# Turning the probabilities of two stick-breaking pairs instead of one with VectorE and DMAs

## The chip, the cores and the metric

The kernel runs on one core of a Trainium2 chip. The metric is the device time of one execution in microseconds (us), lower being better. Before the change the median of 3 runs is 719.0 us (718.34 to 719.76).

## What is computed

A decoder trunk of two layers, for one sequence of 256 tokens of 1024 features, all in float32:

```python
proj = x @ w_in      # q,k,v of 8 stick-breaking heads | q,k,v of 8 MoBA heads | gate_sb | gate_moba
# branch A, per head: stick-breaking, causal, no softmax
z = q @ k.T * scale
log_keep = where(past, log_sigmoid(-z), 0)
suffix = cumsum(log_keep, reverse=True) - log_keep
w = where(past, exp(log_sigmoid(z) + suffix), 0);   o_sb = w @ v
# branch B, per head: with 256 tokens there is one block, so plain causal softmax attention with partial rotary
merged = sigmoid(g_sb) * (o_sb @ w_branch_sb) + sigmoid(g_moba) * (o_mb @ w_branch_moba)
x = layer_norm(ALPHA * x + merged @ w_out)
x = layer_norm(ALPHA * x + (silu(x @ w_gate) * (x @ w_up)) @ w_down)
```

## The kernel before

**Products in three parts.** Each float32 operand is held as two numbers, `hi` and `lo`, so that a product is three matmuls: hi·hi, hi·lo and lo·hi. `split_line` makes the two: ScalarE (ACT) rounds to `hi`, VectorE (DVE) subtracts to `lo`. Weights come as granules of 128 x 1024 numbers (122 a layer): a DMA on SP's queue into one of six `raw` buffers, then ACT to `whi` and DVE to `wlo`, rings of ten slots. Seven granules a layer come over POOL's queue instead. A `raw` load waits until DVE has subtracted the granule that had the buffer before. SP issues its DMAs in order, so a waiting one holds up those behind it.

**The stages of a layer**, named by the matmuls' outputs, `l0` or `l1` ahead: `pv`/`pq` (in layer 1 `pvq`) are v and q projections; `pqk` are q and k of a stick-breaking pair of heads (four pairs, 0 to 3); `pk` and `pu` are k and v of the MoBA heads; `pg` the gates; `pa` and `pb` the two branch projections, four groups each; `pw` the output projection; `pft`, `pf` and `pd` (`pe` at the very end) the feed-forward part. `bankM` hands out two PSUM banks in turn: `pg` of the first gate reuses the bank of the first `pu`, so that it waits until ACT and DVE have split that `pu` into `vmb`. The attention of both branches is woven into these projections.

**A stick-breaking pair** (`sb_line`): scores `sb_s` on TensorE (PE), the mask on DVE, two sigmoids on ACT (`keep` and `beta`), four cumulative products on DVE (`inc`), and `beta = beta * inc` on DVE, which leaves 768 probabilities in each of 128 rows (two heads, 128 + 256 keys). They have to be turned (keys on the partitions) before PE can multiply them with v. Two ways exist:

- `weighted`: six transposes of 128 x 128 on PE into PSUM (`sb_pT`), split by ACT and DVE into `pp`.
- `bounced`: `bounce_line` turns blocks of 32 x 32 on DVE, stores 384 KB to DRAM (`sb_scr`) on SP's queue, loads them back with four DMAs of 96 KB that put the blocks in their places, and ACT and DVE split the result into `pp`.

After either, `both_parts` has four matmuls (`sb_o`), two copies on ACT and four adds on DVE (`sb_f`), and the split into `osb_hi`/`osb_lo`. All pairs share one `pp`, so they pass in order. All MoBA pairs (`mb_...`) bounce; their sums go to `omb_hi`/`omb_lo`, which `pb` reads: its first half (`ks` 0 and 1) takes pairs 0 and 1, the second half pairs 2 and 3. Before the change the stick-breaking pair 3 alone bounces, in each layer.

**The order of the work** is fixed when the program is built. `Weave` keeps a modelled time for PE (`weave.t`), ACT, DVE and POOL; generators (`line()`, `sb_line`, the weight stream) yield the modelled time at which they can go on, and the next one whose time has come issues its instructions. `DMA_ISSUE`, `DMA_STORE` and `DMA_LOAD` are what the model takes for a bounce:

```python
e += DMA_ISSUE          # 2.0
...
nc.sync.dma_start(scr, half)
e += DMA_STORE          # 6.0
...
e += DMA_LOAD[weave.measured]   # 11.0, 13.5
```

So one more step in one place gives another order on every engine around it. The chip then follows that order with semaphores, whatever the model took for granted.

Of the kernel before, what the change touches and what calls it, by code (L numbers as in the profile page):

```python
# [7 lines left out]
F32 = mybir.dt.float32  # L8
F32R = mybir.dt.float32r
# [5 lines left out]
P = 128  # L15
DEPTH = 2
D = 1024
S = 256
# [3 lines left out]
NPAIR = 4  # L22
# [12 lines left out]
class Weave:  # L35
# [12 lines left out]
    def act(self, e, n, f, *args, **kw):  # L48
        f(*args, **kw)  # L49
        self.act_t = max(self.act_t, e) + n / 1200.0 + ACT_FIXED  # L50
        return self.act_t + HOP

    def dve(self, e, n, f, *args, **kw):
        f(*args, **kw)  # L54
        self.dve_t = max(self.dve_t, e) + n / 960.0 + DVE_FIXED
        return self.dve_t + HOP
# [199 lines left out]
ON = (16, 48)  # L256
STATIONARY = ((8, 20), (24, 50), (64, 100), (130, 140), (146, 170), (186, 220))
HOLD = 8
TURNED = ("l0sb3", "l1sb3")
N_WARM = 7  # L260
LEAD = 4
BACKLOG = 0.37
# [15 lines left out]
def hybrid_trunk_kernel(ctx: ExitStack, tc: tile.TileContext, w, xT_in, x_in, ln_in,  # L278
# [11 lines left out]
    page2 = ctx.enter_context(tc.tile_pool(name="page2", bufs=1))  # L290
    acts = ctx.enter_context(tc.tile_pool(name="acts", bufs=12))
    work = ctx.enter_context(tc.tile_pool(name="work", bufs=3))
# [7 lines left out]
    def unit(name, shape, dt=F32):  # L300
        return acts.tile(shape, dt, tag="u4", name=name)
# [4 lines left out]
    def bankM(name, shape):  # L306
        return psM.tile(shape, F32, tag="M", name=name)
# [50 lines left out]
    def split_line(hi, lo, src, n, e):  # L358
        e = act(e, n, nc.scalar.copy, hi, src)
        yield e  # L360
        return dve(e, n, nc.vector.tensor_sub, lo, src, hi.bitcast(F32))
# [51 lines left out]
    hi, lo = (part[:, first[0]] for part in ws.parts[0])  # L413
# [112 lines left out]
    def bounce_line(name, out, half, src, n, e):  # L526

        scr = dram.tile([P, n * P], F32, tag=f"scr{n}", name=f"{name}_scr")
        e = dve(e, n * P, nc.vector.transpose, half.rearrange("p (j n b) -> p n j b", j=4, n=n),
                src.rearrange("p (n j a) -> p n j a", n=n, j=4))  # L530
        e += DMA_ISSUE
        yield e
        nc.sync.dma_start(scr, half)
        e += DMA_STORE
        yield e
        blocks = scr.rearrange("(i a) (j c) -> j a i c", a=32, j=4)
        for j in range(4):
            nc.sync.dma_start(out[32 * j:32 * j + 32].rearrange("a (i c) -> a i c", i=4), blocks[j])
        e += DMA_LOAD[weave.measured]
        yield e  # L540
        return out.rearrange("p (i n b) -> p n i b", i=4, n=n), e

    def blocked(x):
        return x.rearrange("p n (i b) -> p n i b", b=32)
# [34 lines left out]
    def masked(s, m, e):  # L579

        diag = s.rearrange("p h (a c) -> p h a c", c=256)[:, :, :, :P]
        return dve(e, 512, nc.vector.tensor_add, diag, diag,
                   mask[:, m, None, None, :].to_broadcast([P, 2, 2, P]))
# [45 lines left out]
    def bounced(name, p, src, there, v, oT, e, f, own=False):  # L629

        pT, e = yield from bounce_line(name, there, there, src, 6, e)
        if own:
            ws = [pl.tile([P, 2, 384], F32R, tag="T", name=f"{name}_w{i}") for i, pl in enumerate((work, page0))]
        else:
            begun.append(name)
            mine = len(begun)
            while len(summed) < mine:
                yield
            e = max(e, summed[-1])
            yield e  # L640
            ws = [pp[:, i] for i in range(2)]
        e = yield from split_line(*(blocked(x.rearrange("p h (k c) -> p (h k) c", c=P)) for x in ws), pT, 768, e)
        yield from both_parts(name, p, v, oT, e, ws if own else None, f)

    def both_parts(name, p, v, oT, e, ws=None, f=None):

        turns = []
        if ws:  # L650
            yield e + MARGIN
            both = bankB(f"{name}_o", [P, 2, 2, S])
            os = [both[:, h, :1] for h in range(2)]
        else:
            for h in range(2):
                turns.append((yield from turn(e)))
            os = [bankC(f"{name}_o{h}", [P, 2, S]) for h in range(2)]
        pe_after(e)
        for h, o in enumerate(os):
            vs = [x[:, p, 2 * h:2 * h + 2, :].rearrange("p r c -> p (r c)") for x in v]  # L660
            if ws:
                for i, w in enumerate(ws):
                    mm(o[:, 0], vs[0], w[:, h, :S], i == 0, False)
                    mm(o[:, 0, P:], vs[1], w[:, h, S:], False, i == 1)
            else:
                mm(o, vs[0], pp[:, :, h, :S], True, False)
                mm(o[:, :, P:], vs[1], pp[:, :, h, S:], False, True)
        e = pe_done()
        if not ws:
            summed.append(e)  # L670
        yield e
        urgent = f is not None and weave.measured
        weave.held += urgent
        if f is None:
            f = page2.tile([P, S], F32, tag="f", name=f"{name}_f")
        for h, o in enumerate(os):
            e = act(e, S, nc.scalar.copy, f[ROWS[h]], o[ROWS[1 - h], 0, :])
        yield e
        for h, o in enumerate(os):
            for i in range(o.shape[1]):  # L680
                e = dve(e, SUM_COLS[weave.measured], nc.vector.tensor_add, f[ROWS[h]], o[ROWS[h], i, :], f[ROWS[h]])
            if not ws:
                left[turns[h]] = e
        yield e
        outputs.append((yield from split_line(oT[0][:, p, :], oT[1][:, p, :], f, S, e)))
        weave.held -= urgent
# [11 lines left out]
    def sb_line(name, p, s, e, v, oT, done, passed):  # L698
        yield e
        e = masked(s, 0, e)  # L700
        yield e
        def by_head(x):
            return x.rearrange("p (h c) -> p h c", h=2)

        def triple(n):
            return work.tile([P, 768], F32, tag="T", name=f"{name}_{n}")

        there = (page0 if p % 2 else work).tile([P, 768], F32, tag="T", name=f"{name}_keep")
        keep = by_head(there)
        if p % 2 == 0:  # L710
            inc, flat = (by_head(triple("inc")), triple("beta"))
            beta = by_head(flat)
        e1 = act(e, 768, nc.scalar.activation, keep, s[:, :, :384], AF.Sigmoid, scale=-0.125)
        if p % 2:
            while len(passed) < p:
                yield
            inc, flat = (by_head(triple("inc")), triple("beta"))
            beta = by_head(flat)
        e2 = act(e, 768, nc.scalar.activation, beta, s[:, :, :384], AF.Sigmoid, scale=0.125)
        done.append(name)  # L720
        yield e1
        for h, i, a, b in BLOCKS:
            dve(e1, 2 * (b - a), nc.vector.tensor_tensor_scan, inc[:, h, a:b][:, ::-1], keep[:, h, a:b][:, ::-1],
                zero.to_broadcast([P, b - a]), 1.0, OP.mult, OP.add)
        if name == f"l0sb{NPAIR - 1}":
            yield weave.dve_t - 0.3
        e = dve(e2, 768, nc.vector.tensor_mul, beta[:, :, :383], beta[:, :, :383], inc[:, :, 1:])
        passed.append(name)
        if p == NPAIR - 1 and name in TURNED:
            turned.append(e2)  # L730
            yield from bounced(name, p, flat, there, v, oT, e, None)
        else:
            yield from weighted(name, p, beta, v, oT, e)

    def mb_line(name, p, s, e, v, oT, done):
# [19 lines left out]
        for h, i, a, b in BLOCKS:  # L755
            e = dve(e, b - a, nc.vector.tensor_scalar, ex[:, h, a:b], ex[:, h, a:b], rec[:, h, i:i + 1],
                    None, op0=OP.mult)
        if p == 1 and f"{name[:2]}sb3" in TURNED:
            there, f = unit(f"{name}_turn", [P, 1024])[:, :768], None
# [95 lines left out]
    for l in range(DEPTH):  # L855
        G = l * NG_LAYER
        L = f"l{l}"
# [37 lines left out]
        passed, ends, qks = [], {}, {}  # L895

        def sb_pair(p, g):
            hi, lo = (pl.tile([P, 2, S], F32R, tag=f"qk{n}{p % 2}", name=f"{L}qk{n}{p}", bufs=1)
                      for n, pl in (("hi", work), ("lo", page2 if p % 2 else work)))
            ps = bankM(f"{L}pqk{p}", [P, 2, S])  # L900
            feat_major(ps[:, 0, :], g)
            feat_major(ps[:, 1, :], g + 1)
            qks[p] = [(hi[:, i, :], lo[:, i, :]) for i in range(2)]

            def line():
                ends[p] = yield from split_line(hi, lo, ps, 512, pe_done())
                if p % 2:
                    e = max(ends[p - 1], ends[p])
                    yield e + MARGIN
                    yield from two_pairs(sb_line, f"{L}sb", (p - 1, p), (qks[p - 1], qks[p]),  # L910
                                         l * 2 * NPAIR + p - 1, e, sides, v_sb, o_sb, sigmoids, passed)

            sides.append(weave.start(line()))
# [285 lines left out]
```

## Time and profile before

| | |
|---|---|
| median of 3 runs | 719.0 us (718.34 to 719.76) |
| the profiled execution | 718.45 us, of which 716.7 us from its first to its last instruction |
| PE busy | 708.0 us (99%) |
| VectorE busy | 528.3 us (74%) |
| ScalarE busy | 389.3 us (54%) |
| HBM read, written | 148.87 MB, 8.13 MB |
| granted TensorE clock | 0.997 |

A row of the timeline gives start and length in us, engine, line, operation, tiles, shape and count of instructions merged, and in brackets how long the engine had been idle and who ended that. A row of the chain gives start, length and the group of instructions that held the end of the program at that time. Names in rows are without buffer numbers: `l0vmb` stands for both `vmb` tiles of layer 0.

### The profile page before, as it was taken

How to read it: one execution, taken by the hardware profiler on the slowest of the kernel's cores; microseconds unless marked ns; L12 is line 12 of the kernel's file. 1: busy time of each engine (PE TensorE's matmuls, PEld its weight loads, DVE VectorE, ACT ScalarE, POOL GpSimd, SP SyncE). 2: the span in 40 equal slices, each digit the busy share in tenths (PEclk: the TensorE clock that was granted, in tenths of full speed). 3: DMA queues.
4: the chain of work that ended last, by engine and by line, in shares of the span. 5: the costliest groups of instructions: out<-in, count | busy, mean ns of one | idle time of the engine just before them, and what ended most of it. 6: DMA issues, size and time to landing. Idle time of an engine off the chain costs nothing.

```text
span 716.7 us, 12727 instructions
## 1 busy us (share of the span) xinstructions
PE 708.0 (99%) x4981; PEld 651.0 (91%) x4981; DVE 528.3 (74%) x789; ACT 389.3 (54%) x582; POOL 34.6 (5%) x48
## 2 busy tenths in 40 slices
PE   9999999999999999999999999999999999999995
PEld 7889999998899999988889889999888999998885
DVE  5999887898987666643688888879889776665416
ACT  5766677754655545432365567676556554554300
POOL 0001110001000000000000111100010000000001
PEclk9999999999999999999999999999999999999998
DMA  8898889876596555385259589996748855553501
GB/s 291 342 332 248 244 235 252 288 272 228 197 306 231 181 204 196 128 313 187 85 175 347 160 218 242 242 292 207 260 166 282 302 185 196 191 202 99 225 1 59
DMA packets 63053, 157.84 MB, mean 220 GB/s; under 512 B 10896, under 2 KB 23184, under 8 KB 62992
## 3 DMA queue, kind: packets, MB, share of 16 engines
q1 hardware_dynamic: 58304, 142.07, 57.3%
q0 software_dynamic: 4544, 14.68, 9.0%
q8 instruction: 39, 0.64, 0.4%
q10 hardware_dynamic: 144, 0.26, 0.1%
q14 instruction: 22, 0.18, 0.1%
HBM read 148.87 MB, written 8.13 MB: 219 GB/s over the span
## 4 chain that ended last, share of the span: by engine, by line
PE 97%; DMA 1%; SPq 1%; DVE 0%; POOL 0%; POOLq 0%; issue 0%; ACT 0%; DVEq 0%
PE l1pf L442 14%; PE l0pf L442 14%; PE l0pd L442 8%; PE l0pg L442 6%; PE l1pg L442 6%; PE l1pe L442 4%; PE l1pd L442 4%; PE l1pqk L442 3%; PE l1pft L442 3%; PE l0pqk L442 3%; PE l0pw L442 3%; PE l1pvq L442 3%; PE l0pft L442 3%; PE l1pw L442 3%; PE l1pk L442 2%; PE l0pk L442 2%
## 5 line engine op out<-in xcount | busy, mean ns | idle before, releaser
L54 DVE TENSOR_TENSOR wlo<-raw,whi 128x1024 fp32r<-128x1024 f32 (+1 forms) x234 | 277.2, 1202 | 79.6 <-ACT whi L49 76.5
L49 ACT CAST whi<-raw 128x1024 fp32r<-128x1024 f32 (+1 forms) x233 | 237.5, 1036 | 81.5 <-PE l0pd L442 19.4
L442 PE MATMUL l1pf<-xT_hi,whi 128*128 128x256 f32 x288 | 79.6, 276 | 0.0
L442 PE MATMUL l1pf<-xT_hi,wlo 128*128 128x256 f32 x288 | 79.6, 276 | 0.0
L442 PE MATMUL l1pf<-xT_lo,whi 128*128 128x256 f32 x288 | 79.6, 276 | 0.0
L442 PE MATMUL l0pf<-xT_hi,wlo 128*128 128x256 f32 x288 | 79.5, 276 | 0.0
L442 PE MATMUL l0pf<-xT_hi,whi 128*128 128x256 f32 x288 | 79.5, 276 | 0.0
L442 PE MATMUL l0pf<-xT_lo,whi 128*128 128x256 f32 x288 | 79.5, 276 | 0.0
L442 PEld LDWEIGHTS l1pf<-xT_lo,whi 128*128 128x128 f32 x288 | 54.1, 188 | 0.0
L442 PEld LDWEIGHTS l1pf<-xT_hi,whi 128*128 128x128 f32 x288 | 54.1, 188 | 0.0
L442 PEld LDWEIGHTS l1pf<-xT_hi,wlo 128*128 128x128 f32 x288 | 54.1, 188 | 0.0
L442 PEld LDWEIGHTS l0pf<-xT_lo,whi 128*128 128x128 f32 x288 | 54.1, 188 | 0.0
L442 PEld LDWEIGHTS l0pf<-xT_hi,whi 128*128 128x128 f32 x288 | 54.1, 188 | 0.0
L442 PEld LDWEIGHTS l0pf<-xT_hi,wlo 128*128 128x128 f32 x288 | 54.1, 188 | 0.0
L442 PE MATMUL l0pg<-xT_hi,whi 128*128 128x256 f32 x128 | 35.7, 279 | 0.0
L442 PE MATMUL l1pg<-xT_hi,whi 128*128 128x256 f32 x128 | 35.6, 278 | 0.0
L442 PE MATMUL l0pg<-xT_hi,wlo 128*128 128x256 f32 x128 | 35.4, 277 | 0.0
L442 PE MATMUL l0pg<-xT_lo,whi 128*128 128x256 f32 x128 | 35.4, 277 | 0.0
L442 PE MATMUL l1pg<-xT_hi,wlo 128*128 128x256 f32 x128 | 35.4, 277 | 0.0
L442 PE MATMUL l1pg<-xT_lo,whi 128*128 128x256 f32 x128 | 35.4, 276 | 0.0
L442 PE MATMUL l0pd<-whi,l0h_hi 128*128 128x512 f32 x88 | 34.5, 391 | 0.0
L442 PE MATMUL l0pd<-wlo,l0h_hi 128*128 128x512 f32 x88 | 34.3, 389 | 0.0
(371 smaller groups left out, 1781.5 us busy)
## 6 DMA issues: line engine op xcount, KB each, us to landing
raw<-in_w_dram SPq DMA_DIRECT2D x226, 512.0 KB, 4.5
whi<-in_w_dram POOLq DMA_DIRECT2D x14, 512.0 KB, 6.2
wlo<-in_w_dram POOLq DMA_DIRECT2D x14, 512.0 KB, 8.2
ln<-in_ln_dram SPq DMA_DIRECT2D x8, 512.0 KB, 6.0
raw<-in_w_dram SPq DMA_DIRECT2D x7, 256.0 KB, 5.8
l0mb_scr<-l0mb_turn SPq DMA_DIRECT2D x4, 384.0 KB, 7.2
l0mb_turn<-l0mb_scr SPq DMA_DIRECT2D x16, 96.0 KB, 5.3
l1mb_scr<-l1mb_turn SPq DMA_DIRECT2D x4, 384.0 KB, 6.3
```

The source lines that it names most:

```text
L49: f(*args, **kw)
L54: f(*args, **kw)
L442: nc.tensor.matmul(o, a, b, start=start, stop=stop)
```

## The change

`TURNED` names pairs 2 and 3 instead of pair 3 alone, in both layers. Pair 2 has no `keep` buffer that it could be turned into, so it gets a tile of 128 x 1024 (`turn`), in the place (`tag="qk"`) that held q and k of the even pairs; for that, q and k (`hi` and `lo`) of an even pair become one tile.

```diff
-TURNED = ("l0sb3", "l1sb3")
+TURNED = ("l0sb2", "l0sb3", "l1sb2", "l1sb3")
...
-        if p == NPAIR - 1 and name in TURNED:
+        if name in TURNED:
             turned.append(e2)
+            if p == NPAIR - 2:
+                there = work.tile([P, 1024], F32, tag="qk", name=f"{name}_turn", bufs=1)[:, :768]
             yield from bounced(name, p, flat, there, v, oT, e, None)
         else:
             yield from weighted(name, p, beta, v, oT, e)
...
-            hi, lo = (pl.tile([P, 2, S], F32R, tag=f"qk{n}{p % 2}", name=f"{L}qk{n}{p}", bufs=1)
-                      for n, pl in (("hi", work), ("lo", page2 if p % 2 else work)))
+            if p % 2:
+                hi, lo = (pl.tile([P, 2, S], F32R, tag=f"qk{n}", name=f"{L}qk{n}{p}", bufs=1)
+                          for n, pl in (("hi", work), ("lo", page2)))
+            else:
+                both = work.tile([P, 2, 2, S], F32R, tag="qk", name=f"{L}qk{p}", bufs=1)
+                hi, lo = both[:, 0], both[:, 1]
```

What it does to the order is seen at three places of layer 0.

**VectorE, after the cumulative products of pair 2.** `beta` are the finished probabilities, `inc` the cumulative products, `vmb0` the split of the `pu` whose bank the first gate takes. Before:

```order
L54 TENSOR_TENSOR l0sb2_beta_881<-l0sb2_beta_881,l0sb2_inc_880 128x2x383
L54 SCALAR_TENSOR_TENSOR l0sb3_inc_897<-l0sb3_keep_887,zero_104 128x128
L54 SCALAR_TENSOR_TENSOR l0sb3_inc_897<-l0sb3_keep_887,zero_104 128x256
L54 SCALAR_TENSOR_TENSOR l0sb3_inc_897<-l0sb3_keep_887,zero_104 128x128
L54 SCALAR_TENSOR_TENSOR l0sb3_inc_897<-l0sb3_keep_887,zero_104 128x256
L54 TENSOR_TENSOR l0vmb0_802<-l0pu0_804,l0vmb0_802 128x4x128
```

The same place now:

```order
L54 TENSOR_TENSOR l0sb2_beta_879<-l0sb2_beta_879,l0sb2_inc_878 128x2x383
L54 STREAM_TRANSPOSE l0sb2_turn_895<-l0sb2_beta_879 128x6x4x32
L54 SCALAR_TENSOR_TENSOR l0sb3_inc_898<-l0sb3_keep_885,zero_104 128x128
L54 SCALAR_TENSOR_TENSOR l0sb3_inc_898<-l0sb3_keep_885,zero_104 128x256
L54 SCALAR_TENSOR_TENSOR l0sb3_inc_898<-l0sb3_keep_885,zero_104 128x128
L54 SCALAR_TENSOR_TENSOR l0sb3_inc_898<-l0sb3_keep_885,zero_104 128x256
L54 TENSOR_TENSOR l0vmb0_800<-l0pu0_802,l0vmb0_800 128x4x128
```

One transpose of 768 columns now stands between pair 2 and the split `vmb0`; in layer 1 it stands there too, with the last `beta` and the transpose of pair 3 between as well, as before.

**VectorE, at the end of the attention of layer 0.** `l0mb_turn<-l0mb_o` are the sums of MoBA pairs 2 and 3, `l0omb_lo<-l0mb_turn` the splits that `pb` reads, `l0gate` the products with the gates, `wlo` granules of weights. Before:

```order
L54 TENSOR_TENSOR l0gate_1301<-l0gate_1301,l0pa_1686 128x2x256
L54 TENSOR_TENSOR l0mb_turn<-l0mb_o,l0mb_turn 64x256 x2
L54 TENSOR_TENSOR l0omb_lo<-l0mb_turn,l0omb_hi 128x256
L54 TENSOR_TENSOR l0gate_1460<-l0gate_1460,l0pa_1733 128x2x256
L54 TENSOR_TENSOR wlo<-raw_1510,whi 128x1024
L54 TENSOR_TENSOR l0omb_lo<-l0mb_turn,l0omb_hi 128x256
```

Now:

```order
L54 TENSOR_TENSOR l0gate_1283<-l0gate_1283,l0pa_1681 128x2x256
L54 TENSOR_TENSOR l0mb_turn<-l0mb_o_1709,l0mb_turn 64x256 x2
L54 TENSOR_TENSOR l0mb_turn<-l0mb_o_1710,l0mb_turn 64x256 x2
L54 TENSOR_TENSOR wlo<-raw_1450,whi 128x1024
L54 TENSOR_TENSOR l0mb_turn<-l0mb_o,l0mb_turn 64x256 x2
L54 TENSOR_TENSOR l0gate_1443<-l0gate_1443,l0pa_1724 128x2x256
L54 TENSOR_TENSOR wlo<-raw_1505,whi 128x1024
L54 TENSOR_TENSOR wlo<-raw_1553,whi 128x1024
L54 TENSOR_TENSOR l0omb_lo<-l0mb_turn,l0omb_hi 128x256
L54 TENSOR_TENSOR wlo<-raw_1621,whi 128x1024
L54 TENSOR_TENSOR wlo<-raw_1678,whi 128x1024
L54 TENSOR_TENSOR l0omb_lo<-l0mb_turn,l0omb_hi 128x256
```

From the third gate product to the last `omb_lo` there was one granule, and there are five now; the sums of pair 2, which stood ahead of that gate, stand behind it.

**SP's queue in layer 0**, where `l0sb_scr<-l0sb_turn` is the store of pair 2 and `l0sb_scr<-l0sb_keep` that of pair 3. Before:

```order
L138 DMA raw_864<-in_w_dram 128x1024
L138 DMA raw_990<-in_w_dram 128x1024
L533 DMA l0sb_scr<-l0sb_keep 128x768
L135 DMA raw_1052<-in_w_dram 128x2x512
L538 DMA l0sb_keep<-l0sb_scr 32x4x192 x4
L135 DMA raw_1219<-in_w_dram 128x2x512
```

Now:

```order
L138 DMA raw_862<-in_w_dram 128x1024
L533 DMA l0sb_scr<-l0sb_turn 128x768
L533 DMA l0sb_scr<-l0sb_keep 128x768
L538 DMA l0sb_turn<-l0sb_scr 32x4x192 x4
L138 DMA raw_1040<-in_w_dram 128x1024
L538 DMA l0sb_keep<-l0sb_scr 32x4x192 x4
L135 DMA raw_1191<-in_w_dram 128x2x512
```

The fourth granule stood ahead of both the store and the loads, and stands behind two stores and four loads now.

## The prediction

> **What bounds the kernel now.** I read the page's busy times first:
>
> ```profile
> span 716.7 us, 12727 instructions
> ...
> PE 708.0 (99%) x4981; PEld 651.0 (91%) x4981; DVE 528.3 (74%) x789; ACT 389.3 (54%) x582; POOL 34.6 (5%) x48
> ```
>
> PE is all but never idle. Next the view of waits, PE alone:
>
> ```profile
> PE busy L396 <- DVE mhalf L391: 1.0, 1, 1.0
> PE l0pv L442 <- ACT whi L49: 0.2, 1, 0.2
> ```
>
> These two rows, both of the first microseconds, are all that PE waits in the whole program. So the time is the sum of PE's instructions: what leaves PE is gained in full, and what makes PE wait is lost in full. No other engine's busy time counts by itself. Whether a new wait arises is not seen in the view of waits, which has none, but in how late each producer is before PE takes its result; that I read from the timeline.
>
> **What leaves PE.** The chain of work in order of time shows the six transposes of pair 2 in each layer:
>
> ```profile
> 77.56 0.65 PE l0sb_pT L455 x6
> ...
> 427.37 0.66 PE l1sb_pT L455 x6
> ```
>
> 0.65 + 0.66 = 1.31 us go. The four `sb_o` matmuls and the splits into `pp` stay and are only issued later. ACT and DVE read `pp` from SBUF instead of PSUM; neither is PE's time.
>
> **What comes.** Per layer one transpose on DVE, one store of 384 KB, four loads of 96 KB on SP's queue: 0.98 us of DVE a layer (row below) and 0.77 MB through the DMA queues. Both are off PE, so they cost what they delay.
>
> A row-by-row sum that stops here gives 719.0 − 1.3 = 717.7. The Trainium skill speaks against this change: its page "VectorE: DVE Perf Modes", section "Rules for kernel authors", sends a 128 x 128 transpose to TensorE where PSUM may take it, as it may here. By that rule the change isn't made and the time stays 719.0. It weighs the transpose by itself; rows decide here, since PE is the full engine and the question is what DVE's 0.98 us delays.
>
> **First place: the first gate of layer 0.** The added transpose stands ahead of `vmb0`, for which PE's first `l0pg` waits (it takes the same bank). Timeline of DVE, then of PE:
>
> ```profile
> 74.43 0.96 DVE L54 TENSOR_TENSOR l0sb_beta<-l0sb_beta,l0sb_inc 128x766 f32<-128x766 f32 x1
> 75.49 1.91 DVE L54 TENSOR_TENSOR_SCAN l0sb_inc<-l0sb_keep,zero 128x128 f32<-128x128 f32 x4
> 77.31 0.67 DVE L54 TENSOR_TENSOR l0vmb<-l0pu,l0vmb 128x512 fp32r<-128x512 f32 x1
> ...
> 78.87 0.98 DVE L54 STREAM_TRANSPOSE l0sb_keep<-l0sb_beta 128x768 f32<-128x768 f32 x1
> ```
>
> ```profile
> 78.75 0.28 PE L442 MATMUL l0pg<-xT_hi,whi 128*128 128x256 f32 x1
> ```
>
> DVE has no hole here. `beta` ends at 75.39; a transpose of 0.98 from 75.42 ends at 76.40, and the next instruction starts some 0.08 before the end of the one ahead (the scans end at 77.40, `vmb` starts at 77.31), so the scans start at 76.32 instead of 75.49: 0.83 later. `vmb0` then ends at 77.98 + 0.83 = 78.81. Without transposes PE is there at 78.75 − 0.65 = 78.10 and waits 0.76 with the hop: the gate starts at about 78.86, 0.11 later than before. The gain of layer 0 is gone here.
>
> **Second place: the first gate of layer 1.** The same, with the rows of layer 1:
>
> ```profile
> 424.60 0.96 DVE L54 TENSOR_TENSOR l1sb_beta<-l1sb_beta,l1sb_inc 128x766 f32<-128x766 f32 x1
> 425.67 1.90 DVE L54 TENSOR_TENSOR_SCAN l1sb_inc<-l1sb_keep,zero 128x128 f32<-128x128 f32 x4
> ...
> 428.67 0.98 DVE L54 STREAM_TRANSPOSE l1sb_keep<-l1sb_beta 128x768 f32<-128x768 f32 x1
> 429.57 0.65 DVE L54 TENSOR_TENSOR l1vmb<-l1pu,l1vmb 128x512 fp32r<-128x512 f32 x1
> ```
>
> ```profile
> 430.60 0.28 PE L442 MATMUL l1pg<-xT_hi,whi 128*128 128x256 f32 x1
> ```
>
> `beta` ends at 425.56, the transpose at 426.57, the scans start at 426.49, 0.82 later; `vmb` ends at 430.22 + 0.82 = 431.04. PE would be there at 429.94 and goes on at 431.09: a wait of 1.15, and 0.49 later than before. At each place the net lies between −0.65 (DVE's delay hidden) and +0.83 (PE already waiting there, the whole delay added); the rows fix both ends of the wait, so I take the worked values.
>
> **Third place: `pb` of layer 0.** The order shown ahead puts five granules instead of one between the third gate product and the last `omb_lo`. Both DVE and PE start this stretch together: the first gate product waits for the end of `pa`'s first group. DVE's rows of before have every duration:
>
> ```profile
> 128.27 1.79 DVE L54 TENSOR_TENSOR l0mb_f<-l0mb_o,l0mb_f 64x256 f32<-64x256 f32 x4
> 131.87 0.69 DVE L54 TENSOR_TENSOR l0gate<-l0gate,l0pa 128x512 f32<-128x512 f32 x1 [1.81 <-PE l0pa L442]
> 132.73 1.23 DVE L54 TENSOR_TENSOR wlo<-raw,whi 128x1024 fp32r<-128x1024 f32 x1 [0.17 <-ACT whi L49]
> 133.87 0.42 DVE L54 TENSOR_TENSOR l0omb_lo<-l0mb_f,l0omb_hi 128x256 fp32r<-128x256 f32 x1
> 134.21 0.95 DVE L54 TENSOR_TENSOR pp<-l0mb_turn,pp 128x768 fp32r<-128x768 f32 x1
> ...
> 136.81 0.95 DVE L54 TENSOR_TENSOR l0mb_w<-l0mb_turn,l0mb_w 128x768 fp32r<-128x768 f32 x1
> 137.68 1.78 DVE L54 TENSOR_TENSOR l0mb_turn<-l0mb_o,l0mb_turn 64x256 f32<-64x256 f32 x4
> ...
> 140.33 0.86 DVE L54 TENSOR_TENSOR l0mb_turn<-l0mb_o,l0mb_turn 64x256 f32<-64x256 f32 x2
> ...
> 143.41 0.42 DVE L54 TENSOR_TENSOR l0omb_lo<-l0mb_turn,l0omb_hi 128x256 fp32r<-128x256 f32 x1
> ```
>
> In the new order DVE does from the first gate product on: 4 gate products (2.76), `l0mb_f` x4 (1.79, ahead of the gate before), `pp` and `l0mb_w` (1.90), 3 `omb_lo` (1.26), sums x4 and x2 (1.78 + 0.86), and 7 granules (7 x 1.23 = 8.61), before it was 3: 18.96 us in 19 groups. Groups overlap by 0.08 to 0.09 (132.73 + 1.23 is 133.96, the next starts at 133.87), 18 x 0.085 = 1.53. So the last `omb_lo` ends 17.43 us after the gate's start, on before's clock at 131.87 + 17.43 = 149.30. PE does the same matmuls as before between these points:
>
> ```profile
> 129.04 6.80 PE l0pa L442 x60
> 135.85 0.70 PE l0mb_o L442 x4
> 136.54 2.09 PE l0pa L442 x18
> 138.64 0.87 PE l0mb_o L442 x8
> 139.51 2.11 PE l0pa L442 x18
> 141.62 10.88 PE l0pb L442 x96
> ```
>
> `omb_lo` of pair 3 is first read by about the 52nd matmul of `pb` (48 of the first half, three of pair 2, then hi·lo): 141.62 + 52 x 10.88/96 = 147.51. Before, `omb_lo` was ready at 143.83, 3.7 us ahead. Now PE waits 149.30 − 147.51 = 1.8 us. Bounds: 0, since the row of before has the same split 3.7 us early, and 2.3, if six of the overlaps are lost where an instruction waits for the one ahead (6 x 0.085). I take 1.8, worked from the durations themselves. In layer 1 only one granule more than before stands ahead of that split, and I book nothing.
>
> **The moved DMAs.** Pair 2 and pair 3 bounce one behind the other. The rows for pair 3 alone (the DMA view, then SP's timeline):
>
> ```profile
> l0sb_scr<-l0sb_keep SPq DMA_DIRECT2D x1, 384.0 KB, 6.4
> l0sb_keep<-l0sb_scr SPq DMA_DIRECT2D x4, 96.0 KB, 8.3
> ```
>
> ```profile
> 90.41 2.81 SPq L538 DMA_DIRECT2D l0sb_keep<-l0sb_scr  x4
> ```
>
> Pair 2: turned at 76.4, stored by 82.9, loads issued over 2.8 us and landed by about 94. Its four `sb_o` now stand near where pair 3's stood, in the middle of the gates, beyond 104: some 10 us of cover. The granule behind them is loaded 3 to 4 us later, out of a ring of ten. I book nothing, and keep it as a rival.
>
> **The sum.** +0.11 at the first place (−0.65 and a wait of 0.76), +0.49 at the second (−0.66 and 1.15), +1.8 at the third: +2.4 us. The profiled execution took 718.45, which would become 720.85; it is 0.55 under the median of 719.0, so the median goes to 721.4. About 0.2%, 1.4 us, is what a measurement of this kernel can tell from no change: under 717.6 is faster, over 720.4 slower.
>
> **Rivals.**
>
> *The bounce is hidden and nothing waits* (not slower). PE loses its 12 transposes and DVE's delays fall into holes: 719.0 − 1.31 = 717.7. For it: PE waits nowhere today, and the bounce of pair 3 is fully covered. Against it: DVE's rows at the first two places are back to back, and its new order there is certain. It decides if `vmb` ends no later than 78.10 and 429.94. The Trainium skill, page "DMA: Bandwidth & Descriptors", section "Rules for kernel authors", would have it so: issue a DMA early, wait for it late, and its fixed cost overlaps. The trace agrees for pair 3's DMAs, but the rule says nothing of the transpose ahead of `vmb`. Chance 0.12.
>
> *The gates wait, `pb` doesn't.* +0.6 alone: 719.6, no change that can be told. It would need DVE to end the last `omb_lo` 1.8 us sooner than its own durations add up to. Chance 0.15.
>
> *The bounce is late.* DVE's work for pair 2 moves from the stretch of 79 to 90 into the one before the first `l0mb_o`:
>
> ```profile
> 83.54 1.78 DVE L54 TENSOR_TENSOR l0sb_f<-l0sb_o,l0sb_f 64x256 f32<-64x256 f32 x4
> 89.22 0.41 DVE L54 TENSOR_TENSOR l0osb_lo<-l0sb_f,l0osb_hi 128x256 fp32r<-128x256 f32 x1
> ...
> 113.77 1.23 DVE L54 TENSOR_TENSOR wlo<-raw,whi 128x1024 fp32r<-128x1024 f32 x1 [1.29 <-ACT whi L49]
> 118.27 1.22 DVE L54 TENSOR_TENSOR wlo<-raw,whi 128x1024 fp32r<-128x1024 f32 x1 [2.94 <-ACT whi L49]
> 119.41 0.95 DVE L54 TENSOR_TENSOR pp<-l0mb_turn,pp 128x768 fp32r<-128x768 f32 x1
> ```
>
> ```profile
> 121.08 0.70 PE l0mb_o L442 x4
> ```
>
> `pp` (0.95), `sb_f` and `osb_lo` are 3.1 us, the holes are 1.29 + 2.94 = 4.2, and PE takes `pp` 0.7 after it is done (120.36 to 121.08). A granule that lands 2 us later, behind the eight loads, takes more than is left; then `l0mb_o`, and its twin in layer 1, wait 1 to 2.5 us on top: 722.4 to 723.9. Chance 0.18.
>
> **How the numbers follow.** The forecast, with both gates and `pb` waiting, has 0.55: 720.4 to 722.4 by the bounds of the third place (0.8 less, 0.5 more) and a few tenths elsewhere. The range of 8 in 10 reaches down to the case without `pb`'s wait and up over the late bounce: 719.4 to 724.0; it leaves out the hidden bounce. Slower: all of the late bounce and nearly all of the forecast, 0.18 + 0.51 = 0.69. Same: the gates alone, 0.04 of the forecast and 0.08 of the hidden bounce, whose 717.7 lies just inside: 0.27. Faster: 0.04.
>
> **What would show it.** PE's view of waits, empty today, should have `l0pg` and `l1pg` waiting for DVE's `vmb`, 0.8 and 1.1 us, and `l0pb` for `l0omb_lo`, 1.8 us. `l0sb_pT` should count 12 instead of 18. From the first gate product of layer 0 to the last `omb_lo` DVE should run some 17.4 us without a hole; if it takes 15.6 or less, the third term is wrong. `l0mb_o` among PE's waits would be the late bounce. PE's busy time less by 1.3 and no waits would be the hidden one.

## The result, and the profile after

The changed kernel takes 723.5 us in the median of 6 runs (722.96 to 725.39), the kernel before 719.0 beside it (718.21 to 719.76): 1.0070 of its time, 95% interval 1.0058 to 1.0082, so 4.6 us more by the medians. One run of all those below, of the last kernel (best 2), took 1842.74 us and is left out of its ratio. The profiled execution took 725.12 us. Its page first, the span and the busy times:

```profile
span 723.3 us, 12736 instructions
...
PE 709.5 (98%) x4969; PEld 651.3 (90%) x4969; DVE 529.6 (73%) x791; ACT 389.4 (54%) x582; POOL 34.8 (5%) x48
```

PE has 12 instructions less (4981 to 4969) and is nevertheless busy 1.5 us longer. Then the view of waits, PE alone, which was empty behind the first microseconds (columns: us in total, times, longest):

```profile
PE l0pb L442 <- DVE l0omb_lo L54: 2.0, 1, 2.0
PE busy L396 <- DVE mhalf L391: 1.0, 1, 1.0
PE l0pv L442 <- ACT whi L49: 1.0, 1, 1.0
PE l1pg L442 <- DVE l1vmb L54: 1.0, 1, 1.0
PE l0pg L442 <- DVE l0vmb L54: 0.6, 1, 0.6
PE l1mb_s L574 <- ACT l1mb_e L49: 0.5, 1, 0.5
PE l0pq L442 <- ACT whi L49: 0.2, 1, 0.2
```

The three waits that were forecast are there; `l1mb_s` is a fourth, and `l0pv` lies in the first microseconds, which differ from one execution to the next. DVE's timeline of the third place:

```profile
128.92 1.22 DVE L54 TENSOR_TENSOR wlo<-raw,whi 128x1024 fp32r<-128x1024 f32 x1
132.88 0.69 DVE L54 TENSOR_TENSOR l0gate<-l0gate,l0pa 128x512 f32<-128x512 f32 x1 [2.74 <-ACT l0mb_f L49]
...
144.03 0.86 DVE L54 TENSOR_TENSOR l0mb_turn<-l0mb_o,l0mb_turn 64x256 f32<-64x256 f32 x2
144.92 0.69 DVE L54 TENSOR_TENSOR l0gate<-l0gate,l0pa 128x512 f32<-128x512 f32 x1
145.53 2.35 DVE L54 TENSOR_TENSOR wlo<-raw,whi 128x1024 fp32r<-128x1024 f32 x2
147.80 0.42 DVE L54 TENSOR_TENSOR l0omb_lo<-l0mb_turn,l0omb_hi 128x256 fp32r<-128x256 f32 x1
148.13 2.35 DVE L54 TENSOR_TENSOR wlo<-raw,whi 128x1024 fp32r<-128x1024 f32 x2
150.41 0.42 DVE L54 TENSOR_TENSOR l0omb_lo<-l0mb_turn,l0omb_hi 128x256 fp32r<-128x256 f32 x1
```

From the first gate product (132.88) to the end of the last `omb_lo` (150.83) DVE takes 17.95 us without a hole; ahead of that product it stands still for 2.74 us. The row puts the end of that wait down to ACT's copy `l0mb_f`, whose end (132.80) lies 0.02 behind that of `pa`'s first group on PE (132.78); the same product waits for `l0pa` in the kernel before and in the experiment `hole` below, so I read it as a wait for PE here too. What PE does meanwhile:

```profile
148.62 0.28 PE L442 MATMUL l0pb<-l0omb_hi,whi 128*128 128x256 f32 x1
150.88 0.38 PE L442 MATMUL l0pb<-l0omb_lo,whi 128*128 128x256 f32 x1 [1.98 <-DVE l0omb_lo L54]
151.10 0.28 PE L442 MATMUL l0pb<-l0omb_hi,wlo 128*128 128x256 f32 x1
...
151.67 0.41 PE L442 MATMUL l0pb<-l0omb_hi,whi 128*128 128x256 f32 x1
151.88 0.41 PE L442 MATMUL l0pb<-l0omb_lo,whi 128*128 128x256 f32 x1
```

From 151.45 on the matmuls come every 0.21 us instead of 0.11. The table by windows says why: the granted clock is a half (each row: PE, weight load, DVE, ACT and POOL busy, the clock, DMA share, GB/s):

```profile
151.00:151.50 0.50, 0.50 (x5) 0.50 (x6) 0.50 (x1) 0.00 (x0) 0.00 (x0) 0.91 0.85 295
151.50:154.70 3.20, 3.20 (x17) 3.20 (x17) 3.13 (x7) 0.40 (x1) 0.00 (x0) 0.50 0.96 312
154.70:157.00 2.30, 2.30 (x21) 2.30 (x21) 2.30 (x4) 0.41 (x1) 0.00 (x0) 0.97 0.99 328
```

In the trace's clock records the half lasts from 151.41 to 154.82, 3.41 us. It makes PE 1.6 us longer busy (4.27 less 2.66 in the row to `l0pw` below); without it PE would be busy no longer than before.

To see what each place costs I took the start of the first matmul of each named group in PE's timeline and subtracted its start in the kernel before. The table shows by how much this difference grows from one group to the next, for the changed kernel and for the experiments below (us, one profiled execution each):

| stretch | changed | layer 0 only | layer 1 only | tile alone | hold | fill | hold 2 | longer | hole | both | best | best 2 |
|---|---|---|---|---|---|---|---|---|---|---|---|---|
| start to `l0pu` | +0.57 | +0.28 | +0.50 | +0.67 | +0.41 | +0.06 | +0.17 | -0.01 | -0.04 | +0.23 | +0.25 | -0.22 |
| to `l0pg` | +0.07 | +0.07 | 0 | 0 | +0.07 | +0.08 | +0.06 | +0.07 | +0.07 | -0.68 | -0.67 | -0.68 |
| to `l0pb` | +0.37 | +0.33 | 0 | 0 | +0.33 | +0.40 | +0.44 | +0.40 | +0.33 | +0.03 | +0.07 | +0.04 |
| to `l0pw` | +4.27 | +2.66 | 0 | 0 | +0.15 | +2.66 | +0.16 | +6.89 | 0 | +0.17 | 0 | 0 |
| to `l0pft` | 0 | +0.14 | 0 | 0 | +1.57 | +0.13 | +1.45 | 0 | +0.57 | +1.45 | +0.59 | 0 |
| to `l1pu` | +0.01 | -0.04 | 0 | 0 | +0.06 | +0.01 | +0.04 | +0.01 | +0.05 | +0.04 | -0.01 | -0.01 |
| to `l1pg` | +0.47 | 0 | +0.47 | 0 | +0.47 | +0.47 | +0.47 | +0.46 | +0.47 | -0.32 | 0 | 0 |
| to `l1pa` | +0.95 | +0.23 | +0.13 | +0.65 | +0.63 | +0.09 | +1.10 | +1.19 | +0.15 | -0.37 | 0 | +1.71 |
| to `l1pd` | +0.03 | +0.06 | +0.03 | +0.02 | +0.05 | +0.03 | +0.01 | +0.04 | +0.02 | +2.48 | +0.02 | +0.06 |
| all | +6.74 | +3.73 | +1.14 | +1.34 | +3.74 | +3.93 | +3.90 | +9.05 | +1.62 | +3.03 | +0.25 | +0.90 |

The changed kernel's execution is long by its start (0.57) and by the half clock; 6.74 less 0.57 and 1.6 is the median's 4.6. The median is that of runs without the half clock, as far as the mean clock tells: the two in the middle (723.46 and 723.57 us) have 0.996 and 0.998, and the kernel before has 0.996 to 0.998 in its own runs.

### The profile page after: what moved, and what is told of

Read it like the earlier page. It is cut to its first block, busy times and chain, and to the rows that moved or that the text cites. A ratio compares the mean times of both kernels' runs of the same rounds, so it can differ in the third digit from the quotient of the medians.

```text
span 723.3 us, 12736 instructions
## 1 busy us (share of the span) xinstructions
PE 709.5 (98%) x4969; PEld 651.3 (90%) x4969; DVE 529.6 (73%) x791; ACT 389.4 (54%) x582; POOL 34.8 (5%) x48
## 4 chain that ended last, share of the span: by engine, by line
PE 90%; DVE 4%; DMA 3%; ACT 1%; issue 1%; SPq 1%; POOL 0%; POOLq 0%; DVEq 0%
PE l1pf L442 14%; PE l0pf L442 14%; PE l0pd L442 8%; PE l0pg L442 6%; PE l1pe L442 4%; PE l1pd L442 4%; PE l1pg L442 4%; PE l1pqk L442 3%; PE l1pft L442 3%; PE l0pw L442 3%; PE l0pqk L442 3%; PE l1pvq L442 3%; PE l1pw L442 3%; PE l0pft L442 3%; PE l0pk L442 2%; PE l1pk L442 2%
## 5 line engine op out<-in xcount | busy, mean ns | idle before, releaser
L442 PE MATMUL l0pd<-whi,l0h_lo 128*128 128x512 f32 x88 | 34.3, 390 | 0.0
```

What stands on the lines that cost most here:

```text
L442: nc.tensor.matmul(o, a, b, start=start, stop=stop)
```

## Experiments

**One layer at a time, and the tiles alone.** Which part of the change costs what? Three kernels, timed beside the kernel before on one chip:

```diff
-TURNED = ("l0sb2", "l0sb3", "l1sb2", "l1sb3")
+TURNED = ("l0sb2", "l0sb3", "l1sb3")   # layer 0 only
+TURNED = ("l0sb3", "l1sb2", "l1sb3")   # layer 1 only
+TURNED = ("l0sb3", "l1sb3")            # tile alone
```

> Pair 2 goes through DRAM in layer 0 only; layer 1 turns it on TensorE as before the change. My theory, terms that add up by place: of the +4.6 us of both layers, layer 0 makes +2.5 to +3.0 (first gate 0.1, a small wait of l0mb_o 0.3, pb 2.3 or a little more), and in a run whose granted clock falls to a half after the wait of pb 1.7 us more. So 721.5 to 722.0 in most runs, 723.2 to 723.7 in some; l0pb waits 2.0 us for l0omb_lo, l1pg and l1mb_s wait for nothing. Rival, shared traffic or the new tile layout: the cost is not tied to the place, and this kernel has most of the 4.6 us (over 723) or about half of it (721.3) with a wait in the first microseconds.

> Pair 2 goes through DRAM in layer 1 only; layer 0 turns it on TensorE as before the change. My theory: +0.5 at the first gate of layer 1 and +0.8 at the second pair of mb scores, whose bank waits for the exponentials that stand on ACT behind a weight granule's late transfer: 720.2 to 720.4, no half clock after the first microseconds. l1pg waits 1.0 us, l1mb_s 0.5 or more, l0pb for nothing. What I had forecast counts only the first gate: 719.4. Rival, the layout or shared traffic: 721 or more.

> Only the tiles of q and k of the even pairs are laid out as in the changed kernel (hi and lo in one tile); all of pair 2's transposes stay on TensorE. My theory: 719.0, within 0.3 of the kernel before, with PE waiting nowhere. Rival, the layout or the start costs something (the profiled execution of the changed kernel began its second product 0.6 us later): 719.5 or more, with a wait ahead of l0pqk.

Layer 0 alone: 723.09 us against 719.06, ratio 1.0054 (1.0039 to 1.0069), +4.0. Layer 1 alone: 720.01, 1.0015 (1.0007 to 1.0024), +1.0. The tiles alone: 719.66, but by the interval no difference, 0.9999 (0.9990 to 1.0009). The waits stand at the places, so most of the cost is tied to them. The time alone doesn't say so: 723.09 is over the 723 of the rival, and 719.66 is where the rival of the layout stood, with 1.0 us of wait at `l0pq` ahead of `l0pqk` and 0.4 at `l1mb_o`, where I expected none. But `l0pq` waits for nothing in other kernels with the same tiles (fill, hole), so that wait goes with the execution; a layout that costs up to 0.6 us isn't ruled out. PE's waits with layer 0 alone:

```profile
PE l0pb L442 <- DVE l0omb_lo L54: 2.0, 1, 2.0
PE busy L396 <- DVE mhalf L391: 1.0, 1, 1.0
PE l0pg L442 <- DVE l0vmb L54: 0.6, 1, 0.6
```

The wait of `pb` is the same 2.0 us, but in this execution the clock behind it stays whole, by the table of windows:

```profile
151.50:154.70 3.20, 3.20 (x31) 3.20 (x30) 3.13 (x7) 1.33 (x3) 0.00 (x0) 1.00 0.94 320
```

There are 31 matmuls where the changed kernel had 17, and the stretch costs 2.66 instead of 4.27: the half clock is worth 1.6. Of the six runs three have a mean granted clock of 0.994 to 0.996 and take 723.8 to 724.5 us, three have 0.997 and take 722.0 to 722.4; both groups are a few tenths above what I expected, and the median of 723.09 lies between them and stands for neither. In layer 1 alone `l1mb_s` did not wait, against my expectation; in its profile the rows of layer 1 add up to the first gate's 0.47 and little more, and the rest of the +1.0 is not placed.

**Matmuls to fill the wait (fill).** Is the half clock the wait's consequence?

```diff
+            spare = bankC("spare", [P, 2, S])
...
+            for _ in range(12):
+                mm(spare[:, 0, :], ws.take(G + 44)[0][:, :P], o_mb[0][:, 0, :], True, True)
...
         pe_after(outputs[-1])
```

> The changed kernel with twelve matmuls more on PE, into a spare PSUM bank, at the place where l0pb waits for l0omb_lo; their result is read by nobody. They take 12 x 0.113 = 1.4 us of the 2.0 us in which PE stood still. My theory: the wait itself is not made longer, since PE would have stood still for that time; what goes is the half clock behind it, which 1 of 1 profiled execution and about 2 of 6 runs of the changed kernel had and 3 of 6 of the kernel with layer 0 alone. So all runs lie together at 723 to 723.8, none 1.7 to 2 us above the others, and no clock of 0.5 behind pb in the profile. Rival: the two groups of runs come from the start or the DMA queues and stay, 723 and 725; and if PE was not idle there but late, the twelve matmuls add up to 1.4 us: 724.5 and more.

723.66 us against 718.88 (1.0061, 1.0049 to 1.0074). In the profile it does what was expected: PE's timeline shows twelve matmuls and a wait of 0.84 where there were 1.98, and the stretch costs the same 2.66 us as without them.

```profile
147.59 1.52 PE L442 MATMUL spare<-l0omb_hi,whi 128*128 128x256 f32 x12
...
150.41 0.39 PE L442 MATMUL l0pb<-l0omb_lo,whi 128*128 128x256 f32 x1 [0.84 <-DVE l0omb_lo L54]
...
151.58 0.28 PE L442 MATMUL l0pb<-l0omb_lo,whi 128*128 128x256 f32 x1
```

The clock stays 1.00 behind it, and none of its five runs has a mean clock under 0.996. But the runs do not lie together: 722.0 to 724.0. So not all of the spread that I put down to the clock is from it; the first microseconds and layer 1 vary too, and the median (723.66, where the changed kernel has 723.52) shows no gain. That the half clock goes when the wait is cut is seen in the profile and fits the mean clocks; what it is worth in the median is not shown.

**A longer wait (longer).** Two instructions more on DVE ahead of the last `omb_lo`:

```diff
+        if name == "l0mb3":
+            for _ in range(2):
+                nc.vector.tensor_tensor(pp[:, 0], pp[:, 0].bitcast(F32), pp[:, 0].bitcast(F32), op=OP.max)
         outputs.append((yield from split_line(...)))
```

> The changed kernel with two DVE instructions more (a maximum of pp with itself, 768 columns, 0.95 us each) ahead of the last l0omb_lo, so that the wait of l0pb grows from 2.0 to about 3.75 us. My theory: +1.75 us for the wait in every run, and the half clock behind it, in a part of the runs at 2.0 us, in all or nearly all of them: 723.0 + 1.75 + 1.7 = 726.5 to 727.2 in the median, with a clock of 0.5 for 3.4 us in the profile. Rival, the half clock has nothing to do with the length of the wait: two groups as before, most near 725, some near 727; or a longer stretch at half clock, 728.5 or more.

727.46 us (726.74 to 728.32) against 718.88: 1.0121 (1.0107 to 1.0135). The mean clock is 0.992 in all four runs. `l0pb` waits 3.84 us, and the windows show a half clock of 6.83 us, twice 3.41, by the clock records from 150.52 to 157.35:

```profile
150.00:151.00 1.00, 0.00 (x0) 0.00 (x0) 1.00 (x2) 0.59 (x1) 0.00 (x0) 0.76 0.84 307
151.00:152.00 1.00, 0.00 (x0) 0.00 (x0) 1.00 (x2) 0.00 (x0) 0.00 (x0) 0.50 0.88 332
152.00:156.00 4.00, 3.81 (x18) 3.81 (x19) 3.93 (x8) 0.41 (x1) 0.00 (x0) 0.50 0.75 258
```

The stretch to `l0pw` costs 6.89: 2.66, the longer wait (3.84 - 1.98 = 1.86), and 2.4 for the half clock. That the longer wait brings the half clock in every run is shown by the mean clock of the four; the expected 1.7 for it was too little, since it lasted two steps.

**Granules behind the split (hold, hold 2).** What if the last `omb_lo` does not stand behind granules that `pb` does not need?

```diff
-            if g > self.limit:
+            if g > self.limit or g == 48 and weave.outs < 8:
```

> The changed kernel, but the weight granules from the 48th on are held until the last split of layer 0's attention is issued, so three of DVE's granules go behind the last l0omb_lo instead of ahead of it. My theory: the split is ready 3.4 us sooner, l0pb waits for nothing, the clock stays whole, and the time is 2.0 to 2.6 below the changed kernel's median: 720.9 to 721.5, with no run near 725. Rival 1, the held granules then come too late for the output projection behind pb: l0pw waits for wlo instead and the time stays at 723 or is worse. Rival 2, the 2 us wait is not what costs, but the slower clock alone: 721.8 or more.

> The changed kernel with the second of these repairs alone: l0omb_lo ahead of the 48th granule, and the 51st and 52nd granule no longer behind the gate products, which made l0pw wait 1.0 us in the kernel that only held them. My theory: neither l0pb nor l0pw waits; what is left is 0.1 and 0.3 in the gates of layer 0 and 0.6 to 1.4 in layer 1: 720.0 to 720.9, all runs together. Rival, another product behind pb waits for a granule: 721.5 or more.

The first: 722.13 against 719.06 (1.0038, 1.0026 to 1.0050), all five runs within 1.0 us, and above the 720.9 to 721.5 that I expected. `l0pb` no longer waits, but by its view of waits PE now waits behind it, as rival 1 had it for the wait, though not for the time:

```profile
PE l0pw L442 <- DVE wlo L54: 1.0, 1, 1.0
```

The second also exempts the 51st and 52nd granule from the hold that put them behind the gate products: 722.23 against 718.88 (1.0047, 1.0033 to 1.0061). I expected 720.0 to 720.9, and that fell: in the view of waits the wait only has another name.

```profile
PE l0pw L442 <- DVE l0m_lo L54: 0.9, 1, 0.9
```

In both, the stretch to `l0pft` costs 1.5 where that to `l0pw` cost 2.66. Behind the first gate product DVE has so much to do until `pw` that exchanging two pieces of it moves the wait and takes only about 1 us of its cost away.

**Work into the hole ahead of it (hole).** DVE stands still for 2.74 us ahead of that product, with splits queued behind it, of which three have their weights since 124.02 at the latest:

```diff
-            if ahead >= LEAD and (weave.held or ...):
+            if ahead >= LEAD and g not in (43, 44, 45) and (weave.held or ...):
```

> The changed kernel, but three weight granules of layer 0 (the 43rd to 45th, which had landed at 117 to 124 us) are split on ACT and DVE ahead of the first gate product, into the hole of 2.7 us in which DVE waits for the end of pa's first group; behind that product stand three granules ahead of the last l0omb_lo instead of seven. My theory: DVE is not too slow for this stretch, it stands still at its start with its work queued behind a waiting instruction; with the hole filled neither l0pb nor l0pw waits, and what is left is 0.4 us in layer 0's gates and 0.6 to 1.4 in layer 1: 719.9 to 720.9, no half clock. Rival, moving the splits only moves the wait, as holding the granules did (722.2, with l0pw waiting 0.9 us for l0m_lo): 721.7 or more.

720.66 us against 718.94: 1.0023 (1.0014 to 1.0032), inside the 719.9 to 720.9 that I expected. DVE's timeline:

```profile
127.78 3.49 DVE L54 TENSOR_TENSOR wlo<-raw,whi 128x1024 fp32r<-128x1024 f32 x3
131.19 0.42 DVE L54 TENSOR_TENSOR l0omb_lo<-l0mb_f,l0omb_hi 128x256 fp32r<-128x256 f32 x1
132.23 0.69 DVE L54 TENSOR_TENSOR l0gate<-l0gate,l0pa 128x512 f32<-128x512 f32 x1 [0.62 <-PE l0pa L442]
...
145.47 0.42 DVE L54 TENSOR_TENSOR l0omb_lo<-l0mb_turn,l0omb_hi 128x256 fp32r<-128x256 f32 x1
```

The hole is 0.62, the last `omb_lo` is done at 145.89 instead of 150.83, `pb` costs nothing, and `l0pw`, which I expected not to wait, waits 0.3 us for a granule. Of the changed kernel's 4.6 us 2.9 are gone by an order alone, with the same instructions. This settles the third place: DVE was not too slow for it, its work was queued behind an instruction that waits for PE.

**Both repairs (both, best, best 2).** The other two places were forecast to wait since pair 2's transpose stands ahead of `vmb`. So it is held back until `vmb` is issued; the first kernel joins this to hold 2 in both layers, the second to the filled hole with layer 0 alone, and the third splits the 51st and 52nd granule sooner there:

```diff
             if p == NPAIR - 2:
+                yield weave.t + (4.0 if name[1] == "1" else 2.7)
                 there = work.tile(...)
...
+            if ahead >= LEAD and g not in (43, 44, 45, 51, 52) and (weave.held or ...):   # best 2; best: 43 to 45
```

> The changed kernel with two repairs of the order: in both layers pair 2's transpose stands behind the first vmb split on DVE, and in layer 0 both last l0omb_lo stand ahead of the granules from the 48th on, of which the 51st and 52nd are no longer held behind the gate products. My theory: the transposes taken from PE are then worth their 1.31 us less what still waits (l1pg 0.3, l0mb_o 0.3, small waits in layer 1 0.3): 718.3 to 718.9, l0pg and l0pb without a wait. Rival, the bounce of pair 2 starts 2 to 3 us later and is now late for its use: l0mb_o or l1mb_o wait, 720 or more.

> Pair 2 through DRAM in layer 0 only, with that layer's two places repaired: the transpose behind the first vmb split on DVE, and the 43rd to 45th granule in the hole ahead of the first gate product. My theory: nothing in layer 0 waits any more and PE has lost the six transposes, 0.65 us: 718.2 to 718.7, under the kernel before by 0.05 to 0.1 per cent, which five rounds may not tell from no change. Rival, another wait comes up (l0mb_o for pp, or l0pw for a split): 719.2 or more.

> The kernel before this one (layer 0 only, both places repaired), with the 51st and 52nd granule split right behind the last l0omb_lo, since l0pw still waited 0.3 us for such a split there, 0.6 us of time with its small waits. My theory: PE waits nowhere in layer 0 and has lost 0.65 us; the profiled execution, freed of what its first microseconds vary, stands 0.6 below the kernel before, 718.3 to 718.6 in the lowest runs. The one before ran from 718.9 to 723.1, a wider spread than any other; if that comes from the bounce of pair 2, which starts 3 us later behind vmb and lands when it may, this kernel has it too and its median is 719.3 to 720.3, not faster than before; if it was chance, the median is 718.3 to 718.8.

The first: 721.88 against 718.88 (1.0054, 1.0038 to 1.0071), so the 718.3 to 718.9 that I expected is refuted. The first gates do what they should (0.68 gained in layer 0, 0.32 in layer 1), but `l0pw` waits as in the kernel before it, and in layer 1, where pair 3 now bounces ahead of pair 2, `l1pb` waits 0.8 us for `l1omb_lo` (the row to `l1pd` has +2.48).

The second, in layer 0 alone: 720.00 against 718.94 (1.0018, 1.0007 to 1.0029), with 0.3 us of wait left at `l0pw`; its runs go from 718.87 to 723.08 us, and the 718.2 to 718.7 that I expected is missed. The third, with that wait taken away too: 719.61 against 719.18, ratio 1.0002 (0.9991 to 1.0014), inside the 719.3 to 720.3 that I had for the case that the spread is this kernel's own. Its view of waits, PE:

```profile
PE busy L396 <- DVE mhalf L391: 1.0, 1, 1.0
PE l1mb_o L442 <- DVE pp L54: 0.4, 1, 0.4
PE l1pg L442 <- ACT l1gate L49: 0.3, 1, 0.3
PE l0pq L442 <- ACT whi L49: 0.2, 1, 0.2
PE l1sb_o L442 <- DVE pp L54: 0.2, 1, 0.2
```

In layer 0 PE waits nowhere and has gained 0.65 (the rows from `l0pg` to `l1pu` sum to -0.65), which is the price of the six transposes. In layer 1, whose code is that of the kernel before, the same execution lost 1.7 us: the last of pair 3's loads lands at 453.54 us instead of 452.89, although PE began the layer 0.87 us sooner, and `l1sb_o` and `l1mb_o` wait for `pp` behind it. The tiles alone, also with that code, lost 0.65 there. So the gain is seen in the trace and not in the time; no kernel here beats the one before. Why the time doesn't show it stays open (a gain of 0.65 us is just the lower end of the interval): if layer 1 varied alike in both kernels, the 0.65 would remain, and one profile of each can't tell whether it is late more often here.

## Why the prediction was right, and where its sizes were off

**What bounds the kernel** holds: each term is a wait of PE, and the kernel that takes all waits of layer 0 away gains there, in its trace, just what leaves PE. One sentence of it does not: a wait was to be lost in full, and with the half clock more than the wait is lost.

**The first gate of layer 0**: +0.11 forecast, +0.07 measured; a wait of 0.76 forecast, 0.6 in the view of waits. **The first gate of layer 1**: +0.49 forecast, +0.47 measured in seven kernels. These two were worked from DVE's rows in order, and moving the transpose behind `vmb` took them away, as the rival of a hidden bounce would have it.

**`pb` of layer 0** is the term that was mis-sized: 1.8 forecast with 0 to 2.3 as bounds, 2.66 measured with the clock whole, 4.27 with it halved, so both lie above the bounds. DVE took 17.95 us instead of 17.43: at five places an instruction waits for the one ahead and starts 0.03 after its end instead of 0.085 before it, 0.58 in all, and the granules were a little shorter than 1.23. The upper bound had the same half us for six places. The matmul that waits came 2.15 late (150.88 instead of 148.62 + 0.11), within the bounds. The other 0.5 is outside what I worked out: most of it is five matmuls of `pb` that come up to 0.11 late each, two of them at the split of a granule (done at 146.75), two at that of pair 2 (148.22), which were also only just in time, and one right behind the wait. The half clock, 1.6 us in a part of the runs, is no term of the sum at all: I counted a wait by its length, and not by what it leaves behind.

**The bounce's later use** was booked at nothing, and the stretch from `l0pg` to `pb` costs 0.4 in layer 0: the first `l0mb_o` came 0.24 late, as the chain of work of the changed kernel shows:

```profile
123.21 0.94 PE l0mb_o L442 x4
```

DVE's `pp` ended at 123.06 (122.10 + 0.96), and PE, whose last matmul ahead had started at 122.86, would have gone on at 122.97. What made `pp` late was the order and no transfer (timelines of ACT and DVE):

```profile
118.21 1.23 DVE L54 TENSOR_TENSOR wlo<-raw,whi 128x1024 fp32r<-128x1024 f32 x1 [2.40 <-ACT whi L49]
119.35 0.42 DVE L54 TENSOR_TENSOR l0osb_lo<-l0sb_f,l0osb_hi 128x256 fp32r<-128x256 f32 x1
119.88 0.76 ACT L49 COPY l0sb_f<-l0sb_o 64x256 f32<-64x256 f32 x2 [1.70 <-DVE l0osb_lo L54]
122.10 0.96 DVE L54 TENSOR_TENSOR pp<-l0mb_turn,pp 128x768 fp32r<-128x768 f32 x1
```

Two pairs pass here now where one did. Pair 2's `osb_lo` stands behind a granule that DVE splits at 118.21, no later than the granule at that place before (118.27); ACT's copies of pair 3 wait for that `osb_lo`, and DVE's adds and `pp` stand behind them. So DVE's moved work is late at the place that the rival named, by a quarter of a us instead of 1 to 2.5 and too little for the view of waits; a granule that lands late is not what did it.

**A late transfer in layer 1** was not seen. ACT works in order, and ahead of the exponentials stands the negation of a granule that comes over POOL's queue:

```profile
449.23 1.06 ACT L49 ACTIVATE wlo<-whi 128x1024 fp32r<-128x1024 f32 x1 [4.64 <-DMA whi<-in_w_dram]
450.31 1.28 ACT L49 ACT_TABLE_LOAD   x1
451.61 0.37 ACT L49 ACTIVATE l1mb_e<-l1mb_s,l1mb_nmax 128x128 f32<-128x128 f32 x1
```

That transfer was issued at 439.55 and took 9.7 us; in the kernel before it was issued at 434.42 and its negation began 4.5 us later. Now a store and four loads of pair 2 are on their way beside it. The exponentials start 2.4 us after it lands, and the second pair of scores takes their bank. In the seven profiles with this order in layer 1, transfers of 8.1, 8.6 and 8.8 us (hole, layer 1 only, fill) gave no wait of `l1mb_s`, 9.3 (hold) gave 0.2, 9.7, 9.8 and 9.9 (changed, hold 2, longer) gave 0.5, 0.7 and 0.8. An order with the negation behind the exponentials was not tried alone, so this cause rests on the rows, and that the store and the loads beside it make the transfer slow is not shown.

**The sum** was +2.4 and is +4.6: in the profiled execution `pb` with the clock whole makes 0.9 of the difference, the stretch of `l0mb_o` 0.4 and that of layer 1's scores 0.95 (0.1 to 1.2 in other kernels, so that the parts meet so well is in part luck); the half clock's 1.6 comes on top in the runs that have it. The sign and its causes were right. The size was not: 723.5 lies outside the forecast's own 720.4 to 722.4, and the range of 8 in 10 holds it since it was drawn up to the late bounce, which gave a quarter of a us. That part is luck. The Trainium skill's advice that I weighed, to leave a 128 x 128 transpose to TensorE ("VectorE: DVE Perf Modes", "Rules for kernel authors"), pointed the right way: the trace agrees in the result. It does not follow from the transposes' own prices, since with DVE's order repaired layer 0 gains its 0.65 us.

## What to carry to other kernels

When work is moved from a full engine to one with idle time, look where on that engine the idle time lies: a hole ahead of an instruction that waits for the full engine is only filled by what is queued ahead of that instruction, and here 2.7 us of it stood empty while seven splits queued behind it. If exchanging two instructions gives the wait little more than another name, work has to go past the waiting instruction, not around within the queue. Price a new wait of a matmul engine above its length, since the slower clock behind it can cost nearly as much (here 1.6 us behind a wait of 2.0).

## What the runs showed of the hardware

The clock moves in steps of 3.41 us that do not start with the kernel: its first full step begins between 4.22 and 7.23 us after the first instruction in the 13 profiles. In the clock records of all traces here a stretch at one clock within the program lasts a whole multiple of it (3.41, 6.83, 706.56 = 207 x 3.413). In the changed kernel the step from 148.00 to 151.41 held 2.15 us without a new matmul, and the next step was at half clock; with layer 0 alone the same wait fell across a boundary, at 149.39, 0.99 us before it and 1.16 behind, and the clock stayed whole. The step of 2.34 us idle in the longer wait halved it too, and the next one, with 1.67 us idle at half clock, kept it there. The waits of 1.3 us at `l1pg`, which fell within one step in three profiles, never did it. Thus a wait of 2 us seems to cost 2 or 3.6 us by where it falls, which the kernel does not set; that rests on these few profiles and on the two groups of runs with layer 0 alone.

The Trainium skill's page "TensorE: Matmul & The Clock Gate" gives the same free-running window of 3413 ns (section "What's actually happening"); its advice to avoid gaps over about 3 us, in the section "Why this matters for your kernels", is not enough here, where 2.15 us within a window did it.

The first 28 us of one and the same code differ by up to 0.9 us between profiled executions (the first row of the table, whose differences are there by the first `l0pqk`), and the attention of layer 1 by up to 1.7, by when transfers land. That is more than the 0.65 us that a layer can gain by this change.
